# Delta-rule keys: tanh into a PSUM bank, an epsilon on ScalarE, and two matmul steps of a head issued one projection later

## The chip, the cores and the metric

The kernel runs on one core of a Trainium2 chip. The metric is the device time of one execution in microseconds (us), the median of several runs. Five engines work beside each other, each with its own queue of instructions that it takes in order: the matrix engine (PE; its weight loads are shown as PEld), VectorE (DVE), ScalarE (ACT), GpSimd (POOL) and SyncE (SP), which here only issues DMAs. Matmuls write into PSUM, which has 8 banks of 128 x 512 float32; everything else lies in SBUF or in DRAM. An engine that needs another's result waits at a semaphore, and what is queued behind it waits too.

## The reference, cut to what matters

The program is two network blocks one after the other. The change lies in the second block's mixer, in the part that prepares queries, keys and values for the gated delta rule (8 heads of 128 columns, 512 positions, chunks of 64):

```python
qkv = jax.nn.silu(causal_depthwise_conv(qkv, conv_w)).astype(f32)   # conv of width 4
q, k, v = jnp.split(qkv, 3, axis=-1)
q = l2_normalize(to_heads(q)) * (DN_HEAD_DIM ** -0.5)   # x * rsqrt(sum(x*x) + 1e-6)
k = l2_normalize(to_heads(k))
...
k_beta = k * beta[..., None]
v_beta = v * beta[..., None]
a_mat = jnp.where(strict, jnp.einsum("bnhtk,bnhsk->bnhts", k_beta, k) * decay, 0.0) + jnp.eye(DN_CHUNK)
u = solve(a_mat, v_beta)
w = solve(a_mat, k_beta * jnp.exp(g_cum)[..., None])
qk = jnp.einsum("bnhtk,bnhsk->bnhts", q, k) * decay
```

## The kernel before, in words

A float32 product is made of three matmuls on operands split into a high and a low part: high times high, high times low, low times high. A weight tile of 128 x 1024 is loaded by SP (four tiles ahead), its high part `wh` is cast by ACT (L43, two tiles ahead), and the low part `wl` is a subtraction at L44, on VectorE for the tiles dq and dz, on POOL for dv and dk.

The key stage makes, for each head h, seven steps (`dn_keys`, a generator that gives way after each): projection and convolution of k (dk), of q (dq) and of v (dv), each with 24 matmuls at L561; the transposes kt (L1290) with the norm of the keys, which ends in kh; the transposes qt with the norm of the queries; the transposes kn of the normed keys and vt of the values, with the splits kqh and kql; and last kkqk, the products of keys with keys and of queries with keys (12 matmuls, L93 to L95), the decay multiplies and the way out to DRAM (Mp, vk, qqk).

A convolution (`conv4`) is four operations behind the bank that a projection leaves: a scaled copy on ACT (L1279), three multiply-adds on VectorE that read the bank (L1282), a tanh on ACT (L1283) and a multiply on VectorE (L1284) that gives 2x times silu. The factor of 2 is the reason for 4 * EPS in the norms. A norm takes four squares with a sum on ACT (L1326 and L1336), a small tensor_scalar on VectorE that adds the epsilon (L104 within `rstd`, L1338), and a power of -1/2 on POOL (L105, L1339). e1 and e2 at L1311 and L1312 (POOL) and their exponentials (L1318, L1319, ACT) are the decay factors.

The order of the work is written out by hand in `hybrid`: a loop over i calls a step of one head, then of the other, in the order of a tuple. So in one block of the loop head i's projections stand between the later steps of head i-1. Each engine's own queue is made from that order, with some operations moved by a scheduler by priority. In the last block the projections are replaced by "fill" units, which are pieces of a later projection (dz, L1407: 24 matmuls in three pieces of 8). From the block i = 5 on, the operations of `solve[0]` (triangular solves of 16 x 16 blocks, L1391 and L1393, pairs of small VectorE operations that read Mp back from DRAM) are mixed in. Solve 1 follows the key stage, beside the first steps of the chunk preparation (lvA, lvX, lvT).

Of the kernel before, what the change touches and what calls it, by code (L numbers as in the profile page):

```python
# [9 lines left out]
F32 = mybir.dt.float32  # L10
# [3 lines left out]
AF = mybir.ActivationFunctionType  # L14
ALU = mybir.AluOpType
AX = mybir.AxisListType

P = 128
# [6 lines left out]
EPS = 1e-6  # L25


class Net:
# [1245 lines left out]
    def conv4(self, pl, ch, pool):  # L1274
        nc = self.nc
        t = pool.tile([P, TL], F32, name="cv4", tag="cv", bufs=2)
        th = pool.tile([P, TL], F32, name="cvt4", tag="cvt", bufs=6)
        w = [self.hy_cw[:, i * 24 + ch:i * 24 + ch + 1] for i in range(4)]
        nc.scalar.mul(t, pl, w[3])  # L1279
        for i in (0, 1, 2):  # L1280
            n = 3 - i
            nc.vector.scalar_tensor_tensor(t[:, n:], pl[:, :TL - n], w[i], t[:, n:], op0=ALU.mult, op1=ALU.add)  # L1282
        nc.scalar.activation(th, t, AF.Tanh, scale=0.5)  # L1283
        nc.vector.scalar_tensor_tensor(th, th, 1.0, t, op0=ALU.add, op1=ALU.mult)  # L1284
        return th

    def trans4(self, src, name):
# [5 lines left out]
    def dn_keys(self, h, u, bp, S):  # L1293
        nc, a, sc = self.nc, self.a, self.scratch
# [7 lines left out]
        pl, _ = self.colproj(u, w, 1024 + h * P, name="dk")  # L1302
        kf = self.conv4(pl, 8 + h, bp)
        yield
        pl, _ = self.colproj(u, w, h * P, name="dq")
# [8 lines left out]
        pl, _ = self.colproj(u, w, 2048 + h * P, name="dv")  # L1314
# [8 lines left out]
        ss = self.sm.tile([P, 4], F32, name="kss", tag="ss")  # L1323
        junk = bp.tile([P, P], BF16, name="junkk", tag="junk")
        for c in range(4):
            nc.scalar.activation(junk, kt[:, c * P:(c + 1) * P], AF.Square, accum_out=ss[:, c:c + 1])  # L1326
        rk = self.rstd(self.sm, ss, 4, 1.0, 4 * EPS, "rk")
        kh = bp.tile([P, 4, P], F32, name="kh", tag="kh", bufs=2)
        nc.vector.tensor_tensor(kh, v4(kt), rk.unsqueeze(2).to_broadcast([P, 4, P]), op=ALU.mult)
        nc.gpsimd.tensor_tensor(vk[:, :, 1, :], kh, col(self.d_be), op=ALU.mult)  # L1330
# [3 lines left out]
        ssq = self.sm.tile([P, 4], F32, name="qss", tag="ss")  # L1334
        for c in range(4):
            nc.scalar.activation(junk, qt[:, c * P:(c + 1) * P], AF.Square, accum_out=ssq[:, c:c + 1])  # L1336
        m = self.sm.tile([P, 4], F32, name="rqm", tag="rs_m")
        nc.vector.tensor_scalar(m, ssq, 1.0, 4 * EPS, op0=ALU.mult, op1=ALU.add)  # L1338
        nc.gpsimd.tensor_tensor(S["rq"][:, h, :], m, self.mhalf[:, :4], op=ALU.pow)  # L1339
        yield  # L1340
        kq = [bp.tile([P, 4, 2, P], F32R, name="kq" + n, tag="kq" + n) for n in "hl"]
# [227 lines left out]
    def hybrid(self, u, late):  # L1569
        nc, a, sc = self.nc, self.a, self.scratch  # L1570
        with ExitStack() as es:
            cp = self.pool(es, "hyc")
            self.hy_consts(cp)
            with ExitStack() as e2:
                gates = self.hy_gates(u, cp, self.pool(e2, "hg"))
                self.mix(self.sgu(u, cp, late), gates, 0.5)
            S = {}
            dp = self.pool(es, "dnp")
            S["rq"] = dp.tile([P, 8, 4], F32, name="rq")
            fp = self.pool(es, "dnf")  # L1580
            fill = self.dn_fill(u, fp)
            tri = [fp.tile([P, 2, 16, 16], F32, name="s" + n, tag="s" + n) for n in "XT"] + [fp.tile([P, 64], F32, name="sW")]
            ctx, sts = {}, [{} for _ in range(8)]
            prep = [self.dn_prep(h, fp, ctx, sts[h]) for h in range(8)]
            solve = [self.dn_solve(tri, i, *r) for i, r in enumerate(((0, self.BT), (self.BT, 8)))]
            with ExitStack() as e2:
                bp = self.pool(e2, "dnk")
                S["kbuf"] = self.big_tile([P, 2, 6 * TL], F32, "kbuf")
                g = [self.dn_keys(h, u, bp, S) for h in range(8)]
                for i in range(9):  # L1590
                    for h in (i, i - 1, i, i - 1, i, i - 1, i):
                        if 0 <= h < 8:
                            next(g[h])
                        elif h == 8:
                            for _ in range(self.TF):
                                next(fill)
                        if i > 4:
                            for _ in range(self.S0):
                                next(solve[0], None)
                    if i > 7:  # L1600
                        for _ in range(self.PQ):
                            next(prep[0])
                        for _ in range(self.PR):
                            next(prep[1])
            with ExitStack() as e2:
                pp = self.pool(e2, "dns")
                PT = self.big_tile([P, 3, 4, TL], F32, "PT")
                ctx.update(pp=pp, PT=PT)
                scan = [self.dn_scan(h, S, pp, PT[:, h % 3], sts[h], ctx) for h in range(8)]

                def step(gens, i):
                    if 0 <= i < 8:
                        next(gens[i], None)
                A, B = "p1 s0 f s2 s1 p2 f".split(), "s0 p1 s1 f s2 p2".split()
                for i in range(8 - self.PQ):
                    for _ in range(self.S1):
                        next(solve[1], None)
                    step(prep, 0)
                    if i > self.PP:
                        step(prep, 1)  # L1620
                    for _ in range(self.PF):
                        next(fill, None)
                for k in range(10):
                    for i in range(4):
                        if (k, i) == (9, 0):
                            for _ in fill:
                                pass
                            self.bs.close()
                            self.m2, self.slabs = self.pool(self.es, "mraw2", side="right"), 0
                            oh, ol = ctx["og"] = [self.slab([P, KC, TL], F32R, n) for n in ("ogh", "ogl")]  # L1630
                        if k < 2:
                            for _ in range(5):
                                next(solve[1], None)
                        for o in (A, B)[i % 2]:
                            if o == "f":
                                next(fill, None)
                            elif o[0] == "s":
                                step(scan, k - int(o[1]))
                            else:
                                step(prep, k + int(o[1]))  # L1640
            self.mr = self.pool(self.es, "mraw", side="right")
            self.aux = self.pool(es, "aux", 3)
            yt = [self.slab([P, 2, KC, 256], F32R, "yh2") for _ in range(2)]
            for i, tag in enumerate(("sX", "sT", "TU", "TU")):
                n = 1 if i == 3 else 2
                r = fp.tile([P, 2, TL], F32, name="ogr", tag=tag, bufs=2 if i > 1 else 1)
                nc.sync.dma_start(r[:, :n, :], sc["og"][2 * i:2 * i + n].rearrange("h p n -> p h n"))
                self.split(oh[:, 2 * i:2 * i + n, :], ol[:, 2 * i:2 * i + n, :], r[:, :n, :])
            for d in range(KC):
                ds = slice(d * P, (d + 1) * P)  # L1650
                wm = self.weight(a["w_dn_out_2"][0][:, ds].rearrange("(k p) f -> p k f", p=P), [P, KC, P], "wdn")
                g = self.aux.tile([P, 2, TL], F32, name="gys", tag="raw")
                nc.sync.dma_start(g[:, 0, :], sc["gd"][d])
                nc.sync.dma_start(g[:, 1, :], sc["ys"][d])
                pm = self.bank("pdn")
                for kc in range(KC):
                    self.mm3(pm, (wm[0][:, kc, :], wm[1][:, kc, :]), (oh[:, kc, :], ol[:, kc, :]), kc == 0, kc == KC - 1)
                nc.vector.scalar_tensor_tensor(g[:, 0, :], g[:, 0, :], 1.0, pm, op0=ALU.add, op1=ALU.mult)
                nc.vector.tensor_add(g[:, 0, :], g[:, 0, :], g[:, 1, :])
                for i in range(2):  # L1660
                    self.split(yt[i][:, 0, d, :], yt[i][:, 1, d, :], g[:, 0, i * 256:i * 256 + 256])
        return [[yt[t // 2][:, i, :, t % 2 * P:t % 2 * P + P] for i in range(2)] for t in range(4)]
# [781 lines left out]
```

## Time and profile before

| | |
|---|---|
| median of 3 runs | 2586.31 us (2586.13, 2586.31, 2589.76) |
| profiled execution, its own time | 2590.19 us |
| span of it (first to last instruction) | 2588.3 us |
| PE busy | 2459.3 us, 95% |
| VectorE, ACT, POOL busy | 1474.4, 976.7, 473.1 us |
| the key stage in the trace | 1776 to 1976 us |

The trace is of one execution on the slowest core, which here is the only one. "Busy" counts the time in which an engine executes; matmuls overlap each other and their ends are modelled. A row of the waits names the waiting instruction by its output and line, and behind "<-" the one that released it. The granted clock (PEclk) is 1.00 at 2.4 GHz and 0.50 at 1.2 GHz, so 0.93 is a stretch in which PE ran part of the time at the lower one. Line numbers up to 1322 are the same in the changed kernel, and 3 higher in most of what follows.

### The profile page before, as it was taken

What the parts mean: (1) busy time and instruction counts of PE and PEld (TensorE: products, weight loads), DVE (VectorE), ACT (ScalarE), POOL (GpSimd) and SP (SyncE); (2) the same over time, 40 slices, a digit from 0 to 9 for tenths busy, and PEclk for the clock granted to TensorE, in tenths of its full rate; (3) what the DMA queues carried; (4) which work ended last, traced back from release to release, by engine and by line L of the source; (5) the groups of instructions that cost most, each with busy time, mean ns of one, the idle gap of its engine ahead of it and who ended that gap; (6) DMA issues with size and microseconds to landing.
All of it is one profiled execution on the core that took longest, in us unless ns stands there. A gap on an engine that the chain in (4) does not pass through costs nothing. (4 is left out here: it accounts for less than half of the span.)

```text
span 2588.3 us, 32921 instructions
## 1 busy us (share of the span) xinstructions
PE 2459.3 (95%) x12645; PEld 2036.9 (79%) x12645; DVE 1474.4 (57%) x2368; ACT 976.7 (38%) x1761; POOL 473.1 (18%) x481
## 2 busy tenths in 40 slices
PE   7999999998999999999899999999888999996988
PEld 4888888886789989888788887777767888775665
DVE  7554634447557567664533334543676455546899
ACT  4211212125444444433422223444554444323775
POOL 1000000006000000001300001104665423303332
PEclk9999999999999999999999999999998999996999
DMA  7544625444322222145832333437877686754995
GB/s 271 162 151 132 221 66 171 130 148 145 91 79 66 85 67 80 42 155 166 276 107 90 98 94 101 132 91 113 162 153 188 144 184 138 245 202 155 336 333 216
DMA packets 349643, 387.41 MB, mean 150 GB/s; under 512 B 21368, under 2 KB 280925, under 8 KB 349477
## 3 DMA queue, kind: packets, MB, share of 16 engines
q1 hardware_dynamic: 332880, 326.10, 45.0%
q0 software_dynamic: 16416, 59.05, 6.3%
q8 instruction: 102, 1.67, 0.3%
q14 instruction: 65, 0.52, 0.1%
q10 hardware_dynamic: 180, 0.07, 0.0%
HBM read 325.08 MB, written 60.08 MB: 149 GB/s over the span
## 5 line engine op out<-in xcount | busy, mean ns | idle before, releaser
L43 ACT CAST wh<-raw_w 128x1024 fp32r<-128x1024 f32 x132 | 138.2, 1049 | 617.7 <-PE pc L343 232.4
L44 DVE TENSOR_TENSOR wl<-raw_w,wh 128x1024 fp32r<-128x1024 f32 x130 | 159.4, 1228 | 268.7 <-ACT wh L43 265.7
L93 PE MATMUL acc<-wh,gh 128*128 128x512 f32 x440 | 173.9, 395 | 0.0
L94 PE MATMUL acc<-wl,gh 128*128 128x512 f32 x440 | 172.8, 393 | 0.0
L95 PE MATMUL acc<-wh,gl 128*128 128x512 f32 x440 | 172.7, 393 | 0.0
L343 PE MATMUL pa<-u2h,wh 128*128 128x512 f32 (+1 forms) x384 | 144.3, 379 | 5.6 <-ACT u2h L1048 5.6
L343 PE MATMUL pa<-u2h,wl 128*128 128x512 f32 (+1 forms) x384 | 145.3, 379 | 0.0
L343 PE MATMUL pa<-uh,wh 128*128 128x512 f32 x352 | 142.1, 404 | 1.4 <-ACT uh L310 1.4
L343 PE MATMUL pa<-u2l,wh 128*128 128x512 f32 (+1 forms) x384 | 143.2, 374 | 0.0
L343 PE MATMUL pa<-ul,wh 128*128 128x512 f32 x352 | 138.9, 396 | 0.3 <-DVE ul L313 0.2
L343 PE MATMUL pa<-uh,wl 128*128 128x512 f32 x352 | 138.7, 395 | 0.0
L366 DVE TENSOR_TENSOR g<-s,pa 128x512 f32<-128x512 f32 x44 | 30.1, 685 | 140.6 <-PE pa L343 139.9
L343 PE MATMUL pc<-uh,wh 128*128 128x256 f32 x352 | 98.4, 280 | 0.1
L343 PE MATMUL pc<-ul,wh 128*128 128x256 f32 x352 | 98.3, 279 | 0.0
L343 PE MATMUL pc<-uh,wl 128*128 128x256 f32 x352 | 98.2, 279 | 0.0
L95 PEld LDWEIGHTS acc<-wh,gl 128*128 128x128 f32 x440 | 82.7, 188 | 18.8 <-DVE gl L44 0.5
L93 PEld LDWEIGHTS acc<-wh,gh 128*128 128x128 f32 x440 | 83.1, 189 | 18.4 <-ACT s L368 0.2
L94 PEld LDWEIGHTS acc<-wl,gh 128*128 128x128 f32 x440 | 83.1, 189 | 18.4 <-issue 0.2
L2124 DVE TENSOR_TENSOR mwl<-mgu,mwh 128x1024 fp32r<-128x1024 f32 x50 | 81.4, 1637 | 14.6 <-ACT mwh L2123 14.4
L343 PEld LDWEIGHTS pa<-u2h,wh 128*128 128x128 f32 x384 | 72.4, 190 | 19.2 <-ACT u2h L1048 6.1
L343 PEld LDWEIGHTS pa<-u2l,wh 128*128 128x128 f32 x384 | 72.7, 189 | 15.2 <-DVE u2l L1049 0.2
L343 PEld LDWEIGHTS pa<-u2h,wl 128*128 128x128 f32 x384 | 72.6, 189 | 14.6
(944 smaller groups left out, 7187.0 us busy)
## 6 DMA issues: line engine op xcount, KB each, us to landing
raw_ada<-in_w_ada SPq DMA_DIRECT2D x72, 512.0 KB, 4.6
raw_w<-in_w_a SPq DMA_DIRECT2D x66, 512.0 KB, 4.1
raw_w<-in_w_b SPq DMA_DIRECT2D x66, 512.0 KB, 3.9
mdn<-in_expert_w_down SPq DMA_DIRECT2D x16, 1024.0 KB, 7.7
mgu<-in_expert_w_gate SPq DMA_DIRECT2D x16, 1024.0 KB, 7.9
mgu<-in_expert_w_up SPq DMA_DIRECT2D x16, 1024.0 KB, 11.8
raw_wg<-in_w_in SPq DMA_DIRECT2D x16, 512.0 KB, 3.8
raw_wo<-in_w_out SPq DMA_DIRECT2D x16, 512.0 KB, 7.8
```

The source lines that it names most:

```text
L43: self.nc.scalar.copy(hi, src)
L44: (eng or self.nc.vector).tensor_sub(lo, src, hi)
L93: self.nc.tensor.matmul(out, ah, bh, start=start, stop=False)
L94: self.nc.tensor.matmul(out, ah, bl, start=False, stop=False)
L95: self.nc.tensor.matmul(out, al, bh, start=False, stop=stop)
L343: nc.tensor.matmul(dst, w[:, kc, :], u[:, kc, c], start=kc == 0 and wi == 0, stop=kc == KC - 1 and wi == 2)
L366: nc.vector.tensor_mul(g[:, :TL], s[:, :TL], pa[j][1])
L2124: (nc.gpsimd if i == 2 and e < 13 and n >= 4 or n in self.PRE else nc.vector).tensor_sub(l, x, h)
```

## The change

There are three parts. The tanh of a convolution writes back into the projection's PSUM bank and the multiply reads it there (24 instructions). The two epsilon additions of a head are an ACT activation with the bias from a small tile `eps4` (16 instructions), and the power of the key norm is written out where `rstd` was called. And the tuple that orders the steps is another: in a block now come dk of head i, kkqk of head i-2, qt of head i-1, dq and dv of head i, kn and vt of head i-1, kt of head i. So a head's last two steps, (kn, vt) and kkqk, come one projection later than before; the last block has only qt and the rest of two heads, and a tenth block holds kkqk of head 7. Solve 0 begins in the same block i = 5, from its fifth step on.

```diff
--- before.py
+++ after.py
@@ -1280,8 +1280,8 @@
         for i in (0, 1, 2):
             n = 3 - i
             nc.vector.scalar_tensor_tensor(t[:, n:], pl[:, :TL - n], w[i], t[:, n:], op0=ALU.mult, op1=ALU.add)
-        nc.scalar.activation(th, t, AF.Tanh, scale=0.5)
-        nc.vector.scalar_tensor_tensor(th, th, 1.0, t, op0=ALU.add, op1=ALU.mult)
+        nc.scalar.activation(pl, t, AF.Tanh, scale=0.5)
+        nc.vector.scalar_tensor_tensor(th, pl, 1.0, t, op0=ALU.add, op1=ALU.mult)
         return th
 
     def trans4(self, src, name):
@@ -1324,7 +1324,10 @@
         junk = bp.tile([P, P], BF16, name="junkk", tag="junk")
         for c in range(4):
             nc.scalar.activation(junk, kt[:, c * P:(c + 1) * P], AF.Square, accum_out=ss[:, c:c + 1])
-        rk = self.rstd(self.sm, ss, 4, 1.0, 4 * EPS, "rk")
+        m = self.sm.tile([P, 4], F32, name="rkm", tag="rs_m")
+        rk = self.sm.tile([P, 4], F32, name="rkr", tag="rs_r")
+        nc.scalar.activation(m, ss, AF.Identity, bias=self.eps4)
+        nc.gpsimd.tensor_tensor(rk, m, self.mhalf[:, :4], op=ALU.pow)
         kh = bp.tile([P, 4, P], F32, name="kh", tag="kh", bufs=2)
         nc.vector.tensor_tensor(kh, v4(kt), rk.unsqueeze(2).to_broadcast([P, 4, P]), op=ALU.mult)
         nc.gpsimd.tensor_tensor(vk[:, :, 1, :], kh, col(self.d_be), op=ALU.mult)
@@ -1335,7 +1338,7 @@
         for c in range(4):
             nc.scalar.activation(junk, qt[:, c * P:(c + 1) * P], AF.Square, accum_out=ssq[:, c:c + 1])
         m = self.sm.tile([P, 4], F32, name="rqm", tag="rs_m")
-        nc.vector.tensor_scalar(m, ssq, 1.0, 4 * EPS, op0=ALU.mult, op1=ALU.add)
+        nc.scalar.activation(m, ssq, AF.Identity, bias=self.eps4)
         nc.gpsimd.tensor_tensor(S["rq"][:, h, :], m, self.mhalf[:, :4], op=ALU.pow)
         yield
         kq = [bp.tile([P, 4, 2, P], F32R, name="kq" + n, tag="kq" + n) for n in "hl"]
@@ -1577,6 +1580,8 @@
             S = {}
             dp = self.pool(es, "dnp")
             S["rq"] = dp.tile([P, 8, 4], F32, name="rq")
+            self.eps4 = dp.tile([P, 1], F32, name="eps4")
+            nc.gpsimd.memset(self.eps4, 4 * EPS)
             fp = self.pool(es, "dnf")
             fill = self.dn_fill(u, fp)
             tri = [fp.tile([P, 2, 16, 16], F32, name="s" + n, tag="s" + n) for n in "XT"] + [fp.tile([P, 64], F32, name="sW")]
@@ -1587,17 +1592,17 @@
                 bp = self.pool(e2, "dnk")
                 S["kbuf"] = self.big_tile([P, 2, 6 * TL], F32, "kbuf")
                 g = [self.dn_keys(h, u, bp, S) for h in range(8)]
-                for i in range(9):
-                    for h in (i, i - 1, i, i - 1, i, i - 1, i):
+                for i in range(10):
+                    for n, h in enumerate((i, i - 2, i - 1, i, i, i - 1, i) if i < 9 else (8, 7)):
                         if 0 <= h < 8:
                             next(g[h])
                         elif h == 8:
                             for _ in range(self.TF):
                                 next(fill)
-                        if i > 4:
+                        if i > 5 or i == 5 and n > 3:
                             for _ in range(self.S0):
                                 next(solve[0], None)
-                    if i > 7:
+                    if i > 8:
                         for _ in range(self.PQ):
                             next(prep[0])
                         for _ in range(self.PR):
```

How this moves instructions is shown on three pieces. The first two are of VectorE's queue around the seam between two blocks (here heads 3 and 4), before. `cv` is the convolution's sum and `cvt` its result; `kql` is the low part of the normed keys.

```order
L104 TENSOR_SCALAR rkm<-kss 128x4
L44 TENSOR_TENSOR wl<-raw_dq,wh 128x1024
L1284 SCALAR_TENSOR_TENSOR cvt_14852<-cvt_14852,cv_14851 128x512
L1329 TENSOR_TENSOR kh<-kt,rkr 128x512
L1282 SCALAR_TENSOR_TENSOR cv_14938<-dk,cols_13012,cv_14938 128x509
L1282 SCALAR_TENSOR_TENSOR cv_14938<-dk,cols_13012,cv_14938 128x510
L1282 SCALAR_TENSOR_TENSOR cv_14938<-dk,cols_13012,cv_14938 128x511
L1338 TENSOR_SCALAR rqm<-qss 128x4
L1284 SCALAR_TENSOR_TENSOR cvt_14939<-cvt_14939,cv_14938 128x512
L1282 SCALAR_TENSOR_TENSOR cv_14990<-dq,cols_13012,cv_14990 128x509
L1344 TENSOR_TENSOR kql<-kn,kqh 128x4x128
L1282 SCALAR_TENSOR_TENSOR cv_14990<-dq,cols_13012,cv_14990 128x510
```

The same place in the changed kernel:

```order
L1282 SCALAR_TENSOR_TENSOR cv_14786<-dq,cols_13012,cv_14786 128x510
L1282 SCALAR_TENSOR_TENSOR cv_14786<-dq,cols_13012,cv_14786 128x511
L1284 SCALAR_TENSOR_TENSOR cvt_14787<-dq,cv_14786 128x512
L44 TENSOR_TENSOR wl<-raw_dq,wh 128x1024
L1282 SCALAR_TENSOR_TENSOR cv_14831<-dv,cols_13012,cv_14831 128x509
L1347 TENSOR_TENSOR kql<-kn,kqh 128x4x128
L1282 SCALAR_TENSOR_TENSOR cv_14831<-dv,cols_13012,cv_14831 128x510
L1282 SCALAR_TENSOR_TENSOR cv_14831<-dv,cols_13012,cv_14831 128x511
L1332 TENSOR_TENSOR kh<-kt,rkr 128x512
L1284 SCALAR_TENSOR_TENSOR cvt_14832<-dv,cv_14831 128x512
```

The two small operations rkm and rqm have left the queue, L1284 reads the bank (named dq or dv), and kql stands behind the first multiply-add of dv instead of that of dq; kh is ahead of the multiply of dv instead of behind it.

On PE, this is a piece of the difference in the middle of the stage, at the end of a head's dv (which stands ahead of it) and the beginning of the next dk:

```order
-L95 MATMUL kkqk<-kqh,kql 128x256
-L1290 MATMUL kt<-ident,cvt_14321 128x128 x4
+L1290 MATMUL kn<-ident,kh 128x128 x4
+L1290 MATMUL vt<-ident,cvt_14256 128x128 x4
+L1290 MATMUL kt<-ident,cvt_14323 128x128 x4
 L561 MATMUL dk<-hTh,wh 128x512
 L561 MATMUL dk<-hTl,wh 128x512
```

kn and vt of the previous head come in front of kt, and the 12 matmuls of kkqk that stood here are gone from here; they are found behind the 24 matmuls of dk.

The third is PE's queue at the end of the stage, where fill matmuls (dz, L1410 in the changed kernel) take the place of projections:

```order
+L1290 MATMUL kt<-ident,cvt_15578 128x128 x4
+L1410 MATMUL dz<-hTh,wh 128x512
+L1410 MATMUL dz<-hTl,wh 128x512
+L1410 MATMUL dz<-hTh,wl 128x512
+L1410 MATMUL dz<-hTh,wh 128x512
+L1410 MATMUL dz<-hTl,wh 128x512
+L1410 MATMUL dz<-hTh,wl 128x512
+L1410 MATMUL dz<-hTh,wh 128x512
+L1410 MATMUL dz<-hTl,wh 128x512
+L93 MATMUL kkqk<-kqh 128x256 x2
+L1290 MATMUL qt<-ident,cvt_15650 128x128
```

Between kt of head 7 and the first matmuls of kkqk of head 6 there are 8 fill matmuls.

## Rows read from the trace of the kernel before

**Rows 1.** The page's busy times, PE's row: us, share of the span, instructions.

```profile
PE 2459.3 (95%) x12645; PEld 2036.9 (79%) x12645; DVE 1474.4 (57%) x2368; ACT 976.7 (38%) x1761; POOL 473.1 (18%) x481
```

**Rows 2.** Windows: bounds, length, then PE, PEld, DVE, ACT, POOL busy (count), PEclk, DMA.

```profile
1800.00:1825.00 25.00, 25.00 (x125) 20.72 (x124) 15.56 (x25) 14.32 (x42) 14.97 (x12) 1.00 1.02 76
...
1825.00:1850.00 25.00, 21.42 (x99) 17.27 (x98) 18.01 (x24) 15.62 (x45) 19.18 (x16) 0.93 0.90 197
...
1900.00:1925.00 25.00, 18.53 (x89) 15.47 (x88) 23.10 (x50) 8.92 (x24) 12.13 (x10) 0.86 0.72 106
...
1976.00:2000.00 24.00, 17.62 (x93) 13.88 (x92) 11.77 (x28) 4.62 (x9) 7.40 (x6) 0.79 0.75 248
```

**Rows 3.** Waits, 1776 to 1976 us: us in total, times, longest.

```profile
ACT e L1318 <- POOL e L1311: 23.4, 7, 6.9
...
PE kkqk L94 <- DVE kql L1344: 14.2, 5, 6.5
...
PE kn L1290 <- DVE kh L1329: 5.7, 3, 2.4
```

**Rows 4.** Timeline of PE: first matmul of dk_1, dk_2 and the fill behind kt_7.

```profile
1794.28 0.48 PE L561 MATMUL dk<-hTh,wh 128*128 128x512 f32 x1
...
1814.30 0.48 PE L561 MATMUL dk<-hTh,wh 128*128 128x512 f32 x1
...
1963.32 0.48 PE L1407 MATMUL dz<-hTh,wh 128*128 128x512 f32 x1
```

**Rows 5.** Groups by form, 1776 to 1976 us, VectorE: busy, mean ns | idle before.

```profile
L1284 DVE SCALAR_TENSOR_TENSOR cvt<-cvt,cv 128x512 f32<-128x512 f32 x24 | 31.5, 1311 | 22.1 <-ACT cvt L1283 21.5
...
L104 DVE TENSOR_SCALAR rkm<-kss 128x4 f32<-128x4 f32 x8 | 9.0, 1126 | 0.0
...
L1282 DVE SCALAR_TENSOR_TENSOR cv<-dq,cols,cv 128x511 f32<-128x511 f32 x8 | 6.0, 749 | 0.2
...
L1338 DVE TENSOR_SCALAR rqm<-qss 128x4 f32<-128x4 f32 x8 | 1.7, 212 | 0.0
```

**Rows 6.** Timeline near 1907 and 1916 us: two L1284 and POOL's split.

```profile
1907.24 2.35 POOL L44 TENSOR_TENSOR wl<-raw_dk,wh 128x1024 fp32r<-128x1024 f32 x1
...
1907.28 2.86 DVE L1284 SCALAR_TENSOR_TENSOR cvt<-cvt,cv 128x512 f32<-128x512 f32 x1
...
1916.29 0.69 DVE L1284 SCALAR_TENSOR_TENSOR cvt<-cvt,cv 128x512 f32<-128x512 f32 x1
```

**Rows 7.** Groups by form, 1776 to 1976 us, POOL and ACT.

```profile
L44 POOL TENSOR_TENSOR wl<-raw_dv,wh 128x1024 fp32r<-128x1024 f32 x7 | 16.8, 2397 | 3.7 <-ACT wh L43 3.7
...
L1319 ACT ACTIVATE e<-e,d_b 128x128 f32<-128x128 f32 x32 | 12.0, 396 | 9.4 <-POOL e L1312 9.4
...
L105 POOL TENSOR_TENSOR rkr<-rkm,mhalf 128x4 f32<-128x4 f32 x8 | 11.5, 1433 | 2.3 <-DVE rkm L104 2.1
...
L1326 ACT ACTIVATE junkk<-kt 128x128 bf16<-128x128 f32 x32 | 8.9, 278 | 0.7
...
L1339 POOL TENSOR_TENSOR rq<-rqm,mhalf 128x4 f32<-128x4 f32 x8 | 8.6, 1073 | 14.0 <-DVE rqm L1338 14.0
...
L1326 ACT ACTIVATION_READ_ACCUMULATOR junkk<-kt 128x1 f32 x32 | 6.3, 197 | 0.0
```

**Rows 8.** Timeline near the end of the stage: last kkqk, solve 1, PE's wait.

```profile
1973.69 0.28 PE L95 MATMUL kkqk<-kqh,kql 128*128 128x256 f32 x1
...
1987.23 0.18 DVE L1391 TENSOR_TENSOR sW<-sX,sT 128x15 f32<-128x15 f32 x1 [6.36 <-DMA sX<-scr_Mp]
...
1989.93 0.28 PEld L1474 LDWEIGHTS lvA<-TU,Mpl 64*64 64x64 f32 x2 [6.70 <-DVE TU L1468]
```

**Rows 9.** Waits of SP's DMA queue, 1776 to 2000 us: us, times, longest.

```profile
SPq L1383 <- DMA scr_Mp<-kbuf: 66.1, 8, 12.5
```

**Rows 10.** Timeline: last matmul of dv_2, and ACT's copy of its result.

```profile
1836.37 0.40 PE L561 MATMUL dv<-hTh,wl 128*128 128x512 f32 x1
...
1843.67 0.68 ACT L1279 ACTIVATE cv<-dv,cols 128x512 f32<-128x512 f32 x1
```

## The prediction

> **What bounds the kernel now.** I read the page's busy times first: the matrix engine (PE) is busy 95% of the span [rows 1]. So only idle or slowed PE time can be won, and it has to be looked for in the stage that the change touches, the eight key blocks from 1776 to 1976 us. In the stretches of 25 us one sees PE full in the first whole stretch (25.00 of 25.00) and holes afterwards, the worst at 1900 to 1925 with 18.53 us busy and a granted clock of 0.86 [rows 2]. That clock is a mix of the two levels, 2.4 and 1.2 GHz: PE fell to the lower one for a while after a long hole.
>
> Next, the timeline says how long a block of PE work takes. From the first matmul of dk_1 to that of dk_2, with PE never waiting, it is 1814.30 - 1794.28 = 20.0 us. From dk_1 to the first fill matmul (dz) behind kt_7 are seven blocks and 1963.32 - 1794.28 = 169.0 us [rows 4]. Seven clean blocks would be 140.2 us, so **28.8 us** are lost there.
>
> The waits say to what. PE waits 14.2 us at L94 (kkqk) for kql on VectorE, in five waits up to 6.5 us, and 5.7 us at L1290 (kn) for kh [rows 3]: 19.9 us, of which one short wait lies behind kt_7. The rest is clock: the three stretches at 0.93 and the one at 0.86 lack 3 x 0.07 x 25 + 0.14 x 25 = 8.8 us [rows 2]. Together that is the 28.8.
>
> Why kql and kh are late: VectorE is held up by GpSimd (POOL), and ScalarE (ACT) by POOL too (23.4 us at L1318 for the e1 sum) [rows 3]. Two rows in one place show the first: a multiply L1284 starts at 1907.28, 0.04 us behind POOL's weight split (2.35 us), and takes 2.86 us; the next L1284, at 1916.29 with POOL idle, takes 0.69 [rows 6]. The multiply-adds of L1282, with one operand in PSUM, keep a mean of 0.749 us all over the stage [rows 5].
>
> **Part 1, tanh into PSUM.** No instruction is added. ACT's tanh costs about the same, since only its destination changes; I take 0, with bounds of +-0.1 us x 24. The 24 multiplies L1284 take 31.5 us, mean 1.311 [rows 5]. With one operand in PSUM they become like L1282, and I take the free 0.69 [rows 6] for each, as 0.75 would differ by 1.4 us in all: VectorE gets 24 x (1.311 - 0.69) = 14.9 us back, at worst 13.5. None of it is PE time by itself; it counts where L1284 stands ahead of kql or kh.
>
> The row says that a multiply beside POOL ends 0.55 us after POOL does (1907.28 + 2.86 against 1907.24 + 2.35) [rows 6]. The Trainium skill ("SBUF — State Buffer", section "Who interferes with whom") states the rule behind it: VectorE and GpSimd share a port pair as an exclusive lock, whoever issues first keeps it for the whole instruction and the other fully blocks, which cuts both ways. By the row alone VectorE wins; by the rule POOL wins as well, since it no longer waits for a multiply that came first. That has its own time in rival A, where I work it out from rows.
>
> **Part 2, epsilon on ACT.** VectorE loses 8 rkm (L104, 9.0 us) and 8 rqm (L1338, 1.7 us) [rows 5]: 10.7 us, mostly again the wait for POOL (1.126 us mean for 128x4, against 0.212 for the other). ACT gets 16 instructions on 4 columns; the trace has none. The nearest row is the read of a square's sum (128x1, 0.197 us, in the same stage), the far end a 128x128 activation of 0.396 [rows 7]. I take 0.2: 3 us on ACT, 0.4 per block. It has a cost: rkm now stands in ACT's queue behind the four squares, and L1283 of dv behind it. The memset of eps4 is outside the loop: 0.
>
> **Part 3, the order.** kn waits for kh one projection longer than before (24 matmuls at 0.235 us, 5.6 us: 72 of them, 12 shorter ones for kkqk and 16 transposes make the 20.0 us of a block). The longest kn wait was 2.4 us (5.7 in three), so all of it goes. kkqk gets no more distance from kn than before, one projection (dv before, dk now), but VectorE is lighter by 14.9 + 10.7 = 25.6 us in eight blocks, 3.2 per block, and kql stands one place behind the first multiply-add of dv. On SP the wait for Mp (66.1 us in 8 waits [rows 9]) now holds raw_dk, needed a block later, and no longer raw_dq. So what sets the period next?
>
> I find a ring through POOL and ACT. POOL, in order: split of dv, kql of q, Mp issue, e1, qqk issue, rq, e2: 2.40 + 1.29 + 0.82 + 1.36 + 0.56 + 1.07 + 1.31 = 8.8 us (the first is in [rows 7], seven instructions by their means in the stage). ACT, released by e2: four L1319, L1320, dq's copy, two weight casts, the tanh of dq, dv's copy, kqh, four vt copies, four squares, rkm: by their means 9.8, back to back about 8.8 us, as pairs overlap (L1319 first, L1326 last [rows 7]). Then rkr on POOL 1.43, kh 0.69 on VectorE, two products on POOL 1.09 + 1.04, and the next dv split. In sum **21.1 to 22.8 us**, the lower end with rkr at the 1.07 of the same operation at L1339 and with overlaps [rows 7]. PE's own block is 20.0, so PE is no longer late by accident but by 1.1 to 2.8 us per block. I take 21.8: seven blocks are 152.6 us. Against that PE starts with slack, since block 1 ran without a wait; I give 4 us back.
>
> Then three debits. The 30 small operations of solve 0 still have both operands in SBUF and fall into blocks 6 and 7: 3 us, where before they made the 6.5 us wait. kkqk_6 has lost its cover: behind kn_6, vt_6 and kt_7 stand 8 fill matmuls, not 24, so 16 x 0.235 = 3.8 us less (24 take 5.6); I take 3. Clock: shorter waits should leave some 2 us of the 8.8. Blocks 1 to 7: 152.6 - 4 + 3 + 3 + 2 = 156.6 instead of 169.0, a gain of 12.4 us.
>
> The tail is worse. Before, kkqk_7 ends near 1973.8, and PE resumes at 1989.93 after 6.38 us of waiting for TU, which sits in VectorE's queue behind solve 1, and that waits for the last Mp to come back from DRAM (1987.23) [rows 8]. That chain of 16.1 us was covered by 9.7 us of PE work, 19 fill matmuls among it. Now only 8 fill matmuls stand there, so 11 x 0.235 = 2.6 us of cover go; six instead of nine solve operations ahead of TU give 0.7 back. Stall 8.3 instead of 6.4: -1.9 us. The short kn_7 wait (1.3) goes. The clock behind the hole is 0.79 already [rows 2] and stays.
>
> **Sum:** -12.4 - 1.3 + 1.9 = -11.8 us. The profiled execution took 2590.2 us by its own time, 1.9 beyond its span, and the median of the runs is 2586.3, which is 3.9 below it. From the profiled time that is 2578.4; carried to the median, 2574.5. I say 2575.
>
> **Rivals.**
> A. *PE's own limit.* If POOL's operations shrink because nothing of VectorE comes ahead of them (rkr from 1.43 to 1.07, e1 and e2 and the splits by a tenth, 0.7 us), the ring falls to about 20 and PE sets the pace. Then all waits and the clock loss go but the tail's and kkqk_6's: -28.8 - 1.3 + 3 + 1.9 = -25.2, 2561. For it: block 1 ran at 20.0. Against: ACT's 23.4 us of waiting for e1. This is the outcome of the rule of "Who interferes with whom". Chance 0.17.
>
> B. *Nothing measurable.* The ring is at 22.8 us, or the loads are late as before: DMA was busy in 1.02 of the stretch 1800 to 1825 at 76 GB/s [rows 2], and the first raw_dq behind it can hold ACT and so kql_0. Seven blocks at 22.8 are 159.6, with the same debits 167.6 without slack: -1.4 - 1.3 + 1.9, about 2585.5. Chance 0.18, within 0.2%, which is what a measurement of this kernel can tell from no change (5.2 us).
>
> C. *Slower, by ScalarE's queue.* kql needs ACT to reach kqh of kn. Between the end of dv and kkqk stand kn, vt and kt, some 1.2 us, and dk, 5.6. Behind ACT's copy of dv come kqh and kql, with the copy 2.0 us. So ACT may lag 4.8 us behind PE. Before, it did lag by 7: the last matmul of a dv at 1836.37 is followed by its copy at 1843.67 [rows 10]. With rkm, squares and vt copies now between kqh and the tanh of dv, if it kept a lag of 9, six kkqk waits of 4.2 us and one at kkqk_6 of 8.0 (its cover being 3.8 shorter) make 33, and with half of what the clock would lose at 0.86 in every stretch (0.14 x 169 / 2 = 12) 45 us are lost where 28.8 were: 2603. It makes the kernel slower by over 0.2% from a lag of about 7.4 us on (22 + 12 = 34 lost). Against it: PE's wait lets ACT catch up, and the lag of before came at a cast that waited for raw_dq, which SP now issues earlier. Chance 0.08.
>
> D. *The change doesn't do what it says*: L1284 stays at 1.3 us because the lock is asked for by the other SBUF operand and the output. Then only part 2 and the order work: kn's 5.7 and some 2 of kkqk's 14.2 go, the tail's 1.9 comes, 2580. The flat L1282 speaks against it. Chance 0.07.
>
> My forecast has the remaining 0.50. Its own range is 2567 to 2581 (ring 21.1 to 22.4). The range over all reaches to A's and B's times: 2561 to 2588. Faster by over 0.2%: forecast 0.47, A 0.17, D 0.05 = 0.69; within: 0.03 + B's 0.17 + D's 0.02 = 0.22; slower: C and a little of B, 0.09.
>
> **What would show it.** L1284 at 0.7 us in the stage, no 2.8 left. No wait of kn for kh. The spacing of dk_1 to dk_6 at 21 to 22 us, with PE waiting 1 to 2 us per block at kkqk and the name of ACT or POOL behind kql. A wait of about 3 us at kkqk_6 and of 8 at the first 64x64 lvA. The granted clock at 1.00 in most stretches of the stage. Wrong would be a wait on a DMA at kkqk_0, a block above 23 us, or a spacing of 20.0 throughout.

## The result, and the profile after

The changed kernel takes **2614.88 us** (median of 3 runs, 2610.88 to 2615.93) against 2586.31: a ratio of 1.0109, 95% interval 1.0089 to 1.0128. It is slower by 28.6 us where 11 less were forecast. The profiled span is 2613.1 us, 24.8 longer than before.

The first question is where the 24.8 us lie. Three points of the program can be found in both traces: the first matmul of dk_0 (1775.99 before, 1775.81 after), PE's resumption at the first 64x64 lvA (1989.93 [rows 8] and 1993.97), and the first matmul of the projection behind the scan (pdn), by the timelines of before and then after:

```profile
2233.78 1.91 PE L93 MATMUL pdn<-ogh,wh 128*128 128x512 f32 x5 [1.90 <-ACT ogh L43]
```

```profile
2258.61 0.50 PE L93 MATMUL pdn<-ogh,wh 128*128 128x512 f32 x1 [1.89 <-ACT ogh L43]
```

Between the first two the changed kernel takes 4.2 us more, and has done 8 fill matmuls (1.9 us) more by then. Between the second and the third it takes 264.6 instead of 243.9 us: **20.8 us, in a stage that the diff does not touch**, with those 8 matmuls less to do. From there to the end both take 354.5 us.

Stretches of the changed kernel: bounds, length, busy time of PE, PEld, DVE, ACT, POOL with the count of instructions, granted clock, DMA share, GB/s.

```profile
1800.00:1825.00 25.00, 20.35 (x93) 16.42 (x92) 13.22 (x19) 13.64 (x41) 12.28 (x10) 0.92 1.02 76
...
1900.00:1925.00 25.00, 15.66 (x73) 13.00 (x72) 13.65 (x32) 12.93 (x33) 11.73 (x11) 0.77 0.77 149
...
2030.00:2230.00 200.00, 184.76 (x1090) 158.65 (x1088) 117.20 (x218) 79.71 (x204) 60.46 (x55) 0.91 0.68 143
```

The same stretch of the scan before:

```profile
2030.00:2230.00 200.00, 195.88 (x1188) 168.69 (x1187) 110.79 (x230) 87.58 (x226) 71.42 (x67) 0.97 0.70 162
```

In 200 us of the scan PE is busy 184.76 us instead of 195.88, and its clock is 0.91 instead of 0.97. So it loses 11 us by standing still and 0.06 x 200 = 12 us by running part of the time at 1.2 instead of 2.4 GHz. Together that is the 23 us (20.8, and 1.9 of work that was done before).

What PE waits for there stands for the most part in one row for each kernel (us in total, times, longest), before and then after; the changed kernel waits another 2.4 us in shorter waits, 1.8 of them at uw for Ul on VectorE:

```profile
PE lvA L1474 <- DVE TU L1468: 4.0, 6, 1.6
```

```profile
PE lvA L1477 <- DVE TU L1471: 12.7, 6, 2.6
```

Six times, once for each of the heads 2 to 7, PE reaches the 64x64 lvA and waits for TU on VectorE: about 0.5 us before (the last one 1.6); after, 0.9 at the first, 2.6 at the next four and 1.4 at the last. One of these places in detail, in the trace of before (start, length, instruction, idle time ahead and what ended it):

```profile
2084.70 0.29 DVE L44 TENSOR_TENSOR Sl<-ST,Sh 128x128 fp32r<-128x128 f32 x1 [0.36 <-ACT Sh L43]
...
2085.01 0.43 DVE L44 TENSOR_TENSOR c3l<-PT,c3h 128x256 fp32r<-128x256 f32 x1
...
2086.10 0.55 DVE L44 TENSOR_TENSOR c3l<-PT,c3h 128x384 fp32r<-128x384 f32 x1
...
2087.89 0.69 DVE L1468 TENSOR_TENSOR TU<-TU,lvX 128x512 f32<-128x512 f32 x1 [0.65 <-PE lvX L1456]
...
2087.89 2.35 POOL L44 TENSOR_TENSOR wl<-raw_vk,wh 128x1024 fp32r<-128x1024 f32 x1 [6.46 <-ACT wh L43]
...
2088.63 0.33 PE L1474 MATMUL lvA<-TU,Mpl 64*64 64x64 f32 x2 [0.49 <-DVE TU L1468]
```

and the same place of a head in the changed kernel:

```profile
2099.43 2.40 POOL L44 TENSOR_TENSOR wl<-raw_vk,wh 128x1024 fp32r<-128x1024 f32 x1 [3.17 <-ACT wh L43]
...
2100.06 1.91 DVE L44 TENSOR_TENSOR Sl<-ST,Sh 128x128 fp32r<-128x128 f32 x1 [0.90 <-ACT Sh L43]
...
2101.79 1.32 POOL L1440 TENSOR_TENSOR gst<-gst,ysl 128x512 f32<-128x512 f32 x1
...
2101.90 1.49 DVE L44 TENSOR_TENSOR c3l<-PT,c3h 128x256 fp32r<-128x256 f32 x1
...
2103.18 1.33 POOL L1441 TENSOR_TENSOR ysl<-gst,ysl 128x512 f32<-128x512 f32 x1
...
2103.91 1.02 DVE L44 TENSOR_TENSOR c3l<-PT,c3h 128x384 fp32r<-128x384 f32 x1
...
2105.45 0.67 DVE L1471 TENSOR_TENSOR TU<-TU,lvX 128x512 f32<-128x512 f32 x1
...
2106.18 0.32 PE L1477 MATMUL lvA<-TU,Mpl 64*64 64x64 f32 x2 [2.58 <-DVE TU L1471]
```

The reader is to see POOL's rows. Before, the split of vk starts at 2087.89, when VectorE is just at the subtraction that PE waits for; the small splits ahead of it (Sl and two c3l) took 0.29, 0.43 and 0.55 us. After, the same split starts 6 us ahead of TU, and the two products of a gsg unit (L1440, L1441) follow: Sl takes 1.91, one c3l 1.49 and the other 1.02 us, each ending 0.1 to 0.4 us behind a POOL operation. This place is no exception: over the 200 us an Sl of 128x128 takes 783 ns in the mean, where it took 365. The Trainium skill ("SBUF — State Buffer", section "Who interferes with whom") says that the pair of ports which VectorE and GpSimd share is an exclusive lock for a whole instruction; these rows agree, but for overlaps of 0.2 us.

Why the products stand elsewhere: a fill unit is 8 of a projection's 24 matmuls, and the unit that ends a projection also issues its way out on ACT and POOL. A head of the scan takes six units, which are exactly two projections, so each head meets the units in the same phase. The changed loop has five units in the key stage, where the old one had four (the tuple of the tenth block begins with 8, which means a unit). All later units come one earlier, in every head.

The key stage itself: groups by form of the changed kernel (busy, mean ns of one | idle before), and PE's waits from 1776 to 1976 us.

```profile
L1284 DVE SCALAR_TENSOR_TENSOR cvt<-dk,cv 128x512 f32<-128x512 f32 x8 | 5.5, 691 | 27.6 <-ACT dk L1283 27.6
...
L1330 POOL TENSOR_TENSOR rkr<-rkm,mhalf 128x4 f32<-128x4 f32 x8 | 8.3, 1042 | 4.2 <-ACT rkm L1329 4.2
...
L1329 ACT ACTIVATE rkm<-kss,eps 128x4 f32<-128x4 f32 x8 | 2.4, 300 | 0.2
...
L1341 ACT ACTIVATE rqm<-qss,eps 128x4 f32<-128x4 f32 x8 | 2.4, 298 | 0.3
```

```profile
PE kkqk L93 <- ACT kqh L1346: 11.8, 4, 5.7
...
PE kkqk L94 <- DVE kql L1347: 10.3, 7, 3.6
```

L1284 is at 0.69 us in all 24 places, and no wait of kn for kh is left; but PE waits 11.8 us at L93 for kqh on ACT, and 10.3 at L94 for kql, in sum 22 us where it was 21.6 (14.2 and 5.7 [rows 3], and 1.7 in this row of before).

```profile
PE kkqk L93 <- ACT kqh L1343: 1.7, 3, 0.7
```

The block starts in the middle of the stage of the changed kernel:

```profile
1839.76 0.48 PE L561 MATMUL dk<-hTh,wh 128*128 128x512 f32 x1
...
1861.20 0.48 PE L561 MATMUL dk<-hTh,wh 128*128 128x512 f32 x1
...
1882.97 0.48 PE L561 MATMUL dk<-hTh,wh 128*128 128x512 f32 x1
...
1905.43 0.48 PE L561 MATMUL dk<-hTh,wh 128*128 128x512 f32 x1
```

They are 21.44, 21.77 and 22.46 us apart. Two other blocks are far longer, 27.4 us (dk_2 to dk_3) and 32.7 (dk_6 to dk_7), and these rows say why, with the last wait of the stage:

```profile
1819.70 1.04 ACT L43 CAST wh<-raw_dq 128x1024 fp32r<-128x1024 f32 x1 [5.66 <-DMA raw_dq<-in_w_in]
...
1821.86 0.58 PE L93 MATMUL kkqk<-kqh 128*128 128x256 f32 x1 [3.69 <-ACT kqh L1346]
...
1911.63 0.18 DVE L1394 TENSOR_TENSOR sW<-sX,sT 128x15 f32<-128x15 f32 x1 [7.92 <-DMA sX<-scr_Mp]
...
1917.02 0.58 PE L93 MATMUL kkqk<-kqh 128*128 128x256 f32 x1 [5.75 <-ACT kqh L1346]
...
1921.19 0.55 PE L94 MATMUL kkqk<-kql,kqh 128*128 128x256 f32 x1 [3.59 <-DVE kql L1347]
...
1993.97 0.47 PE L1477 MATMUL lvA<-TU,Mpl 64*64 64x64 f32 x2 [8.26 <-DVE TU L1471]
```

### The profile page after: what moved, and what is told of

The parts are those of the page before. It is cut to its first block, busy times and chain, and to the rows that moved or that the text cites. A ratio compares the mean times of both kernels' runs of the same rounds, so it can differ in the third digit from the quotient of the medians.

```text
span 2613.1 us, 32906 instructions
## 1 busy us (share of the span) xinstructions
PE 2469.4 (95%) x12645; PEld 2045.5 (78%) x12645; DVE 1471.6 (56%) x2352; ACT 983.3 (38%) x1777; POOL 472.3 (18%) x482
## 5 line engine op out<-in xcount | busy, mean ns | idle before, releaser
L44 DVE TENSOR_TENSOR wl<-raw_w,wh 128x1024 fp32r<-128x1024 f32 x130 | 159.5, 1229 | 268.4 <-ACT wh L43 265.4
L93 PE MATMUL acc<-wh,gh 128*128 128x512 f32 x440 | 173.7, 395 | 0.0
L94 PE MATMUL acc<-wl,gh 128*128 128x512 f32 x440 | 172.8, 393 | 0.0
L93 PEld LDWEIGHTS acc<-wh,gh 128*128 128x128 f32 x440 | 83.0, 189 | 18.5 <-ACT s L368 0.2
L94 PEld LDWEIGHTS acc<-wl,gh 128*128 128x128 f32 x440 | 82.9, 188 | 18.2 <-issue 0.2
L2129 DVE TENSOR_TENSOR mwl<-mgu,mwh 128x1024 fp32r<-128x1024 f32 x50 | 81.5, 1639 | 14.4 <-ACT mwh L2128 14.2
```

What stands on the lines that cost most here:

```text
L44: (eng or self.nc.vector).tensor_sub(lo, src, hi)
L93: self.nc.tensor.matmul(out, ah, bh, start=start, stop=False)
L94: self.nc.tensor.matmul(out, ah, bl, start=False, stop=False)
L2129: (nc.gpsimd if i == 2 and e < 13 and n >= 4 or n in self.PRE else nc.vector).tensor_sub(l, x, h)
```

## The experiments

Each was timed beside runs of the kernel before on the same chip; "before" is the median of those runs, and the interval is that of the ratio.

**e1, the order without the fifth unit.**

```diff
-                    for n, h in enumerate((i, i - 2, i - 1, i, i, i - 1, i) if i < 9 else (8, 7)):
+                    for n, h in enumerate((i, i - 2, i - 1, i, i, i - 1, i) if i < 9 else (9, 7)):
```

> The changed kernel with one fill unit less in the key stage (four, as before; the tenth block issues kkqk of head 7 alone). Theory P (the fifth fill unit shifts every later fill unit by one in the scan, so that other GpSimd operations meet VectorE's): the waits at the 64x64 lvA after 2030 us fall from 2.6 us to about 0.5 each, heads are about 26 us apart instead of 30, and the time is about 20 us shorter, 2595. Rival Q (the later waits come from the order of the keys itself, by late Mp, vk or qqk data): no difference by more than 3 us, 2612 to 2618.

Measured: 2594.02 us, before 2590.69, ratio 1.0016 (0.9996 to 1.0037). The scan's waits are those of before:

```profile
PE lvA L1477 <- DVE TU L1471: 4.1, 6, 1.6
```

**e2, the fifth unit alone, in the kernel before.**

```diff
                     if i > 7:
+                        for _ in range(self.TF):
+                            next(fill)
                         for _ in range(self.PQ):
```

> The kernel before with a fifth fill unit at the end of the key stage, nothing else. Theory P: the scan shows the waits of about 2.6 us at the 64x64 lvA and the time is about 2606 (20 us more than before). Rival Q: within 3 us of before, 2583 to 2590.

Measured: 2609.62 us, before 2590.69, ratio 1.0081 (1.0051 to 1.0110).

```profile
PE lvA L1474 <- DVE TU L1468: 12.7, 6, 2.6
```

One more unit makes the kernel before slower by 19 us, with the same 12.7 us of waits as in the changed kernel; taking it away from the changed kernel takes all but 3 us of the loss, and e1's interval does not tell these 3 us from none. That the fifth unit makes the loss is shown from both sides, and Q falls. That it does so by collisions with GpSimd, the rest of theory P, is left to e8.

**e3, parts 1 and 2 alone; e6, part 3 alone.** e3 is the diff without its last hunk, e6 the last hunk alone.

> The kernel before with parts 1 and 2 alone (tanh into PSUM, epsilon on ScalarE), in the old order. Theory P: the scan is as before, 0.5 us waits. In the key stage VectorE is lighter by about 25 us, so part of the waits for kql (14.2 us) and kh (5.7 us) goes: 2575 to 2583. Rival R (the key stage is bound by the ring through GpSimd and ScalarE whatever VectorE does): no difference by over 3 us, 2583 to 2590.

Measured: 2590.33 us, before 2590.69, ratio 0.9999 (0.9980 to 1.0018). The time is the one that rival R gave; the rows do not settle R's reason. PE's waits in the key stage:

```profile
PE kkqk L94 <- DVE kql L1347: 8.6, 6, 4.6
...
PE kkqk L93 <- ACT kqh L1346: 5.9, 4, 2.9
...
PE kn L1290 <- DVE kh L1332: 4.2, 3, 2.2
```

With VectorE lighter (its busy time from 1776 to 1976 is 123.8 us, 135.1 before) the wait for kql falls from 14.2 to 8.6 and that for kh from 5.7 to 4.2, but a wait for kqh on ACT rises from 1.7 to 5.9. The 3 us that are left of it are lost in a longer wait at the end of the stage (9.34 us for the solve instead of 6.38). Differences of this size can't be told from one trace each: from dk_1 to the fill behind kt_7 e3 takes 164.6 us and the kernel before 169.0, but the same code of before takes 166.4 in the trace of e2 and 166.0 in that of e10.

What is far from chance is another row. VectorE is lighter by 11 us only, not by the 25.6 that the prediction took off, since the subtraction at L44, with two operands in SBUF, now takes longer. For the tile dq, from 1776 to 1976 us, before and then e3:

```profile
L44 DVE TENSOR_TENSOR wl<-raw_dq,wh 128x1024 fp32r<-128x1024 f32 x7 | 8.5, 1214 | 15.6 <-ACT wh L43 15.6
```

```profile
L44 DVE TENSOR_TENSOR wl<-raw_dq,wh 128x1024 fp32r<-128x1024 f32 x7 | 15.5, 2210 | 15.6 <-ACT wh L43 15.6
```

Its mean is 1.21 us in the traces of e2 and e10 too, and 2.47 and 2.33 in those of e11 and e13, which have parts 1 and 2 in the old order. With dz (6.4 us before, 9.6 in e3) 10 us of the relief came back in this way.

> The kernel before with part 3 alone (new order with five fill units, tanh in SBUF, epsilon on VectorE). Theory P: the scan waits of 2.6 us are there, and the key stage is longer than in the changed kernel by what VectorE loses: 2615 to 2630. Rival Q': if parts 1 and 2 made the loss, this one is near before, 2580 to 2592.

Measured: 2618.59 us, before 2590.69, ratio 1.0105 (1.0060 to 1.0149). The loss comes with the order and its fifth unit; parts 1 and 2 have no share that can be measured.

**e8, which POOL operations do it.** The changed kernel without the two products of a gsg unit, whose gate its result lacks.

```diff
             nc.scalar.activation(t, pl, AF.Tanh, scale=0.5)
-            nc.gpsimd.tensor_tensor(t, t, y, op=ALU.mult)
-            nc.gpsimd.tensor_tensor(y, t, y, op=ALU.add)
             nc.gpsimd.dma_start(sc["ys"][d], y)
```

> The changed kernel (five fill units) without the two GpSimd products of a gsg unit (their gate is left out of the result). Theory P' (these two products and the GpSimd split of vk hold up VectorE's operations ahead of the subtraction from TU): two of three collisions go, the wait at the 64x64 lvA falls from 2.6 to about 1.1 us, and the time by about 10 us, to about 2605. Rival U (the matmuls in front of the wait are too few, or data come late): the wait stays at 2.6 us and the time above 2611.

Measured: 2598.11 us, before 2586.79, ratio 1.0039 (1.0019 to 1.0060); more than was expected. The timeline holds its own control: at one of these waits (2079.95) the unit is still one of z, whose products remain, and at the next it is gsg.

```profile
2076.26 2.44 DVE L44 TENSOR_TENSOR c3l<-PT,c3h 128x256 fp32r<-128x256 f32 x2
...
2079.95 0.33 PE L1475 MATMUL lvA<-TU,Mpl 64*64 64x64 f32 x2 [2.60 <-DVE TU L1469]
...
2104.03 1.92 DVE L44 TENSOR_TENSOR Sl<-ST,Sh 128x128 fp32r<-128x128 f32 x1 [0.90 <-ACT Sh L43]
...
2105.87 0.41 DVE L44 TENSOR_TENSOR c3l<-PT,c3h 128x256 fp32r<-128x256 f32 x1
...
2106.81 0.54 DVE L44 TENSOR_TENSOR c3l<-PT,c3h 128x384 fp32r<-128x384 f32 x1
...
2108.60 0.32 PE L1475 MATMUL lvA<-TU,Mpl 64*64 64x64 f32 x2 [1.03 <-DVE TU L1469]
```

With products left (at 2076) the two c3l take 2.44 us in sum and PE waits 2.60, as in the changed kernel. Without them they take 0.41 and 0.54, and PE waits 1.03; the 1.92 us of Sl beside the split of vk stay. So the wait comes from the collisions, and not from too few matmuls ahead of it. The products are gone from every gsg unit (POOL is busy 50.4 us of the 200 from 2030 on, 60.5 in the changed kernel), so the time also holds what they cost elsewhere.

**e10, a third phase.** The kernel before with three units in the key stage.

```diff
-                    for h in (i, i - 1, i, i - 1, i, i - 1, i):
+                    for h in (i, i - 1, i, i - 1, i, i - 1, i if i < 8 else -1):
```

> The kernel before with three fill units in the key stage instead of four. Theory P (what counts is which unit falls where in a head of the scan, period six units for each head): a third phase, so the waits at the 64x64 lvA differ from both 0.49 and 2.6 us or take one of these, and the time moves with them: between 2570 and 2615. Rival V (five units were bad only because a unit was used up too early): three are as good as four or better, 2580 to 2591, waits of 0.5 us.

Measured: 2587.29 us, before 2586.79, ratio 0.9998 (0.9984 to 1.0013). From 2030 us on there is no wait at lvA at all, and others (scK, 4.3 us) in its place. So of the three phases tried two take the same time, and five units is the bad one. That agrees with P and with V's time; it tells less than e8 did.

**e7, the solve behind kh of head 5 (four units).** VectorE's queue is made by a scheduler. In the changed kernel it put the first solve operation (1911.63) in front of head 5's first multiply-add of dq (1911.94), though the loop begins the solve behind dv of head 5. So besides a later begin in the loop there is a tie, a copy of one column into the solve's tile:

```diff
+        if h == 5:
+            nc.vector.tensor_copy(S["sW"][:, 0:1], kh[:, 0, 0:1])
...
-                        if i > 5 or i == 5 and n > 3:
+                        if i > 5:
```

> The changed kernel with four fill units, and solve 0 tied to come behind kh of head 5 (one extra copy of one column into sW). In e1 VectorE stood still in front of the first solve operation for Mp of head 3, and kkqk_4 waited 7.84 + 3.62 us. Theory S (the new order sends Mp out a projection later while the solve stays where it was): these two waits fall below 4 us in total, the clock stays up there, and the time is 8 to 13 us under e1 (2594.0): 2581 to 2586. Rival T (the ring through GpSimd and ScalarE is late there anyway): the wait stays above 8 us, the time within 3 us of e1.

Measured: 2588.53 us, before 2586.79, ratio 1.0019 (1.0005 to 1.0033), against e1's 1.0016: the 8 to 13 us of S are not there. (The traced execution of e7 took 2581.33 us, less than its median.) The two waits of e1,

```profile
1922.92 0.58 PE L93 MATMUL kkqk<-kqh 128*128 128x256 f32 x1 [7.84 <-ACT kqh L1346]
...
1927.12 0.55 PE L94 MATMUL kkqk<-kql,kqh 128*128 128x256 f32 x1 [3.62 <-DVE kql L1347]
```

are gone at kkqk_4, but a block later the solve makes kt wait and kkqk after it:

```profile
1921.63 0.71 PE L1290 MATMUL kt<-ident,cvt 128*128 128x128 f32 x3 [3.59 <-DVE sT L1398]
...
1932.90 0.55 PE L94 MATMUL kkqk<-kql,kqh 128*128 128x256 f32 x1 [3.36 <-DVE kql L1349]
```

11.5 us became 7.0. S was right on the cause of the wait at kkqk_4 and wrong on what its going is worth: the 30 small operations cost PE a wait in the next block too, and the time does not show the difference.

**e9, two units ahead of kkqk_6**, on top of e7: the ninth block's tuple is (8, 8, 6, 7, 8, 7, 8).

> As e7, and two of the four fill units stand ahead of kkqk of head 6 instead of one. Theory: the wait at kkqk_6, 5.86 us in e1, falls by the 1.9 us that 8 matmuls take, or to 4 us; the time is 1 to 3 us under e7, 2579 to 2585. Rival: the units are missing behind it (qt, kn of head 7, the end of the stage), and the time is that of e7 within 2 us.

Measured: 2587.16 us, before 2586.79, ratio 1.0008 (0.9996 to 1.0021). The wait at kkqk_6 is 2.79 + 1.16 us instead of 4.09 + 0.54 in e7; the end of the stage gives it back (7.48 instead of 5.08 at the first lvA). Not resolved from e7.

**e11, e12, e13, less POOL in the ring.** The low part of q is put on VectorE (`FL = "gv"` instead of `"qgv"`) in e3 (e11) and in e9 (e12); e13 is e11 with the product of L1347 moved too (`FL = "v"`).

> e3 (parts 1 and 2, old order, four fill units) and the low part of q (L1346, 1.3 us on GpSimd) on VectorE. Theory W (the key blocks follow the ring through GpSimd and ScalarE, so only work taken out of the ring helps): blocks 3 to 5 fall by about 1 us each from e3's 22.9 and 21.6, the time by 3 to 8 us from 2590, to 2583 to 2587. Rival X (GpSimd is not in the ring, or the operation on VectorE collides with it and costs the same): 2588 to 2593.

> e9 (all three parts, four fill units two of which cover kkqk_6, late solve) and the low part of q on VectorE. Theory W: blocks 3 to 5 fall from 24.1, 20.5 and 21.8 towards 20.5, the time by 3 to 8 us from 2587, to 2579 to 2584. Rival X: 2585 to 2590.

> e11 and the product for qqk (L1347, 1.3 us on GpSimd) on VectorE too. Theory W: another 0 to 1 us per block, as this product lies beside ScalarE's part of the ring; 2581 to 2587. Rival X: more operations with two SBUF operands on VectorE meet the GpSimd splits; kql comes later and the time is 2588 to 2595.

Measured: 2583.98, 2583.30 and 2583.84 us, before 2586.90; ratios 0.9992 (0.9973 to 1.0011), 0.9985 (0.9966 to 1.0004), 0.9993 (0.9978 to 1.0008). The medians lie in the ranges that W gave, but no interval excludes no change, and the kernel before itself took 3.8 us less beside them than beside e3 (2586.90 against 2590.69). By the ratios e11 is 1.8 us under e3, less than W's 3, and e12 6 us under e9. In the traces the seven blocks from dk_1 on take 163.0 us in e11 (164.6 in e3), which is within the spread of such traces, and 160.2 in e12 (164.8 in e9). The blocks that W named bear it out in part: in e11 22.9 became 22.0, but 21.6 became 25.0, in a block that takes 21.6 to 26.4 us in the traces of before, e2 and e10; in e12 24.1 became 21.1, and the other two stayed within 0.3 us.

**e14, e12 once more.**

> e12 again, word for word, in five rounds, since it is the only version whose interval lies almost wholly under 1 (0.9966 to 1.0004). If the gain is real: a ratio to before of 0.997 to 0.9995 with the interval under 1. If e12 was chance: a ratio within 0.999 to 1.002.

Measured: 2581.68 us, before 2585.86, ratio 0.9990 (0.9978 to 1.0003); the seven blocks take 160.7 us, as in e12. A version that beats the kernel before isn't shown; if e12 does, it is by some 0.1 or 0.2%.

## Why the prediction was wrong

**The step that failed is the end of the sum.** It counted the parts to the first lvA and took all behind as it was. Fill matmuls were counted as cover, ahead of kkqk_6 and behind kkqk_7, but not the units in the stage, five in place of four: "every later unit comes one earlier" was no term, and no rival had it. e2 prices it at 19 us of the 28.6, e1 at 21 (2614.88 less 2594.02, not timed beside each other; by the ratios they give 21 and 24). Rival C, the one on the slow side, had another mechanism (ACT's lag in the key stage) and another place. But the fifth unit isn't all: e1, which lacks it, is no faster than the kernel before, so the gain of 11.8 us failed by itself, in the key stage.

**The key stage was missed by a smaller sum.** From dk_1 to the fill behind kt_7 it took 164.8 us (169.0 before, forecast 156.6). But kkqk_6, 1.5 us, and its waits, 3.2, have moved out of that stretch, and the forecast has both in it. Like for like it is 169.5. That is no gain on the trace of before, and a loss against those of e2 and e10, where the same code takes 166.4 and 166.0 us; so some 3 us of the 12.4 to be won were the chance of one trace (its block from dk_4 to dk_5 took 26.4 us, 21.8 and 21.6 in the others). The 169.5 are 12.9 us above the forecast. About half of these 12.9 lies in the first two blocks (46.0 us from dk_1 to dk_3, where 2 x 21.8 - 4 = 39.6 were forecast) and half in the last two with kkqk_6 (57.8, where 43.6 + 3 + 3 + 2 = 51.6 were). The three between took 65.7, forecast 65.4. Term by term:

- L1284: forecast 0.69, measured 0.69 (1.311 before [rows 5]). Right. Also rkr on POOL, 1.433 before [rows 7], is 1.042, as rival A had it (1.312 in e3, with the old order); the ring didn't fall to 20 by that.
- VectorE's relief: forecast 25.6 us; e3 shows 11, the changed kernel 16 (135.1 to 117.2, less 1.7 of kkqk_7's operations that have moved out). The sum took L44 and the solve's small operations as they were, and these, with two SBUF operands, now take longer (14.9 to 17.9 us and 9.4 to 14.1 in the changed kernel).
- rkm and rqm on ACT: forecast 0.2, measured 0.30.
- kn's wait for kh: gone, as forecast.
- The ring: forecast 21.1 to 22.8, taken 21.8; the three blocks that nothing else disturbs have 21.4, 21.8 and 22.5. Right, and with PE waiting 1.2 to 2.0 us per block. That it is POOL that binds is supported (ACT waits 34.2 us at L1318 for POOL's sum, 23.4 before; e12 takes 160.2 us for the seven blocks and e9 164.8) and not settled: in e11 the blocks of W did not all become shorter, and no time leaves the noise.
- The 4 us of slack at the start: wrong sign. ACT waited 5.66 us for a raw_dq to arrive (1819.70), and kkqk_0 waited 3.69 + 0.96 us. This was part of rival B ("the first raw_dq"), and stood among the signs of error. The rows say so; no run took this wait away.
- The solve: forecast 3 us, measured 5.75 + 3.59 at kkqk_4, and a clock of 0.77 from 1900 to 1925 beside it. VectorE stood 7.92 us in front of the first solve operation, since Mp of head 3 now leaves a projection later. It is an added wait: what is queued behind it was not listed. e7 moved it, at no gain in time.
- kkqk_6: forecast 3, measured 1.93 + 1.23. The wait at the end of the stage: forecast 8.3, measured 8.26. Right.
- Clock: forecast 2 us lost, measured about 12, more than the 8.8 of before: 0.92 and 0.77 in the two stretches above, and 0.94, 0.96 and 0.93 in three more of the eight.

So the size of the ring was right, and what it should give (12 us) was spent by two waits that the ring does not know, raw_dq and the solve, and by the clock after them. e3 says besides that a VectorE with 11 us less of busy time in the stage gives nothing in the old order that can be measured: the time is the same to 0.2%.

## What to carry to other kernels

When a loop hands out pieces of another stage's work as filler, count the pieces before and after: one more or one less shifts all that follow, and in a loop whose period is a multiple of the pieces it does so in each round. Follow what a moved step writes to the reader at the far end (here Mp to the solve), as its queue waits there. And price the relief of an engine with what comes next on it: in e3 10 of the 25.6 us came back in the next operation with two SBUF operands, and the time did not move.

## What the runs showed of the hardware

In the scan 11 us more of idle PE came with 12 us more of loss by the clock, though no wait there was over 2.6 us, and the old ones of 0.5 to 1.6 us left the clock at 0.97. The length of the waits isn't all that counts: in the same 200 us of e10 PE stood still as long as before (4.4 us, 4.1 before), in three waits of 1.0 to 1.9 us, and the clock was 0.99. And GpSimd operations one behind the other slow VectorE operations of two SBUF operands one after the other: 0.29, 0.43 and 0.55 us became 1.91, 1.49 and 1.02 beside operations of 2.40, 1.32 and 1.33.
